# Three edits in the SSD part of a float32 trunk: a borrowed bank for the sums of squares, one output piece in another place, and phase buffers 64 bytes lower

## The chip, the cores and the metric

The kernel runs on one core of one Trainium2 chip. The metric is the device time of one execution in microseconds (us); three runs of the kernel before gave a median of 1430.0 us (1429.96 to 1431.1). PE is the matrix engine TensorE, PEld its weight loads, DVE is VectorE, ACT is ScalarE, POOL is GpSimd, SP is SyncE, which issues the DMAs.

## The reference

Two layers over 512 tokens of width 1024 in float32; the first mixes tokens with an SSD (Mamba-2), the second with an HGRN2. After each mixer come a layer norm, a squared-ReLU MLP of width 4096, a second layer norm and a gate:

```
for i in range(2):
    mix = ssd_mixer(x, ...) if i == 0 else hgrn2_mixer(x, ...)
    h = layer_norm(ALPHA * x + mix)
    h = layer_norm(ALPHA * h + relu(h @ w1)**2 @ w2)
    x = h + sigmoid(h @ w_gate) * (p[i] @ w_proj)
```

The change lies in the SSD mixer. It projects x to z, xs, B, C and dt; xs, B and C pass through a causal convolution of width 4 and a silu. With 32 heads of 64 values in 4 groups, and chunks of 128 tokens:

```
y = y_diag + y_off + d_skip * xs           # products within a chunk, and from the state before it
y = y * silu(z)
y = rms_norm(y, over each group of 512 values) * norm_w
mix = y @ w_out
```

## The kernel before, in words

**Numbers.** Each float32 operand of a large product is split into two parts, hi and lo, of a reduced type that the matrix engine reads at full speed, and a product is three matmuls: hi*hi, hi*lo, lo*hi (`mm3`, L116 to L118). A weight (`unit`) is 128 x 1024: SP loads it into one of three `raw` buffers, ACT casts it to `whi` (L110), DVE subtracts to get `wlo` (L112); there are six `whi` and six `wlo` buffers. The activations that the products read lie in the nine large buffers of pool `b8` (in the profile they are called `b`), or, in the MLP, in tiles called `blk`. In the profile `out<-moving,stationary` names the two operands of a matmul: the stationary one has been loaded into the array, the moving one streams through.

**Phases.** The program goes through four phases: ssd, mlp0, hgrn, mlp1. Each opens a pool of scratch buffers at the same SBUF address (`begin`). Ahead of it in the layout lies `pad`, 64 bytes per partition that nothing reads; one GpSimd memset fills it at the start. So all phase buffers start at byte 173568 of a partition, which is a multiple of 512. The `blk` tiles are the first two buffers of the mlp phases (173568 and 181760). The buffers of `b8`, `whi`, `wlo`, `raw` and the accumulator all start 192 bytes past a multiple of 256.

**PSUM.** Eight banks: four for `pj` (projections, output pieces), one `pt`, two `py0` and `py1`, one `pm`.

**The SSD loop.** Heads are worked on in 16 tiles j of 128 rows (two heads), in pairs. `x_part(j)` projects a tile of xs (24 matmuls) and runs the convolution on it: ACT L570, three DVE instructions L573 that all read the bank, ACT's Silu L574. `z_part(j)` projects a tile of z and takes its Silu (L622). `turn_pair(k)` transposes the two xs tiles of pair k on PE (L639) into `pt` and `pm`; DVE L643 and L647 read them. `decays` prepares the decay factors (ACT's Exp, DVE L663 to L670), `states` the chunk states (L679, DVE L681 to L686). `mixed(j)` makes the tile's y in `py0` (even j) or `py1` (odd j) (L696, L698), and `finish(j)` reads that bank (DVE L714), multiplies by silu(z), splits and adds to the sum of squares `ss` of its group (L724).

When a group g of four tiles is finished, `rms_group(g, bank)` sums `ss` over its rows with four small matmuls (L729; eight records in the profile), ACT takes a square root from the bank (L731), DVE the reciprocal `ri` (L732). `pieces(g, ri)` is a generator of eight output pieces; a piece is 12 matmuls into a fresh `pj` bank, and DVE L250 scales it by `ri` and adds it to `acc`, after which the bank is free. `some(n)` draws n pieces. In iterations k = 3, 5 and 7 (of 1 to 8), `x_part` of tiles 2k and 2k+1 comes first, then `rms_group` with a fourth `pj` bank, then in k = 3 and 5 four pieces at once. In k = 7 there follow z_part(12), mixed(12), mixed(13) and turn_pair(7); the eight pieces of that group are drawn in k = 8, four after z_part(15) and four after the last `mixed`.

**Order.** PE's order in this part is as written (a manual schedule). Within each other engine a scheduler orders the instructions by priorities, where a `high_priority` offset pulls a block ahead of its place (`LEAD` 100, `SOON` 40, `SUMS` for the block sums of the MLP). In the MLP `weight_sums` (L311) loads eight tiles `r` and forms sums of weight blocks on DVE (L323 to L329); the lead of the first such block is `SUMS[0]`.

Of the kernel before, what the change touches and what calls it, by code (L numbers as in the profile page):

```python
# [15 lines left out]
P = 128  # L16
# [13 lines left out]
TURN = 200  # L30

PERIODS = ("TTTTTTTT",) + 3 * ("TTQTQTQTQTQTQTQ",) + ("QQQQQQQ",)
SUMS = (150, 300, 300, 300)

JOBS = "q0 q1 v0 q2 q3 g0 q4 q5 v1 q6 q7 g1 o".split()
LEADIN = 6.0
# [5 lines left out]
def trunk(ctx: ExitStack, tc, a):  # L42
    nc = tc.nc
    pool = lambda name, bufs, **kw: ctx.enter_context(tc.tile_pool(name=name, bufs=bufs, **kw))
# [5 lines left out]
    accp = pool("accp", 1)  # L50
    w4 = pool("w4", 2)
    sm = pool("sm", 2)
    pad = pool("pad", 1)
    psj = pool("psj", 4, space=PSUM)
    pst = pool("pst", 1, space=PSUM)
    psy = pool("psy", 1, space=PSUM)
# [4 lines left out]
    def nm(s):  # L61
        uid[0] += 1
        return f"{s}_{uid[0]}"

    def mk(p, shape, tag, dt=F32, **kw):
        return p.tile(list(shape), dt, tag=tag, name=nm(tag), **kw)
# [9 lines left out]
    def begin(name):  # L76

        if phase:
            phase[1].__exit__(None, None, None)
            phase.clear()  # L80
        phase.append(tc.tile_pool(name=name, bufs=1, reuse_waits="tile"))
        phase.append(phase[0].__enter__())
        phase.reverse()
        phase.append(bufs[name])

    def tmp(tag, shape, dt=F32):
        return mk(phase[0], shape, tag, dt, bufs=phase[2].get(tag, 1))

    def bank(p, tag):
        return mk(p, [P, T], tag)  # L90
# [8 lines left out]
    def unit(src, lead=LEAD):  # L99
        n = src.shape[1]  # L100
        with tc.high_priority(offset=lead):
            raw = mk(raws, [P, 1024], "raw")
            nc.sync.dma_start(raw[:, :n], src)
        return split(raw[:, :n], lead)
# [33 lines left out]
            mm3(ps[:m, tok], hi[:, c], lo[:, c], xs.h(k, tok), xs.l(k, tok), k == 0, k == 7)  # L138


    nc.gpsimd.memset(mk(pad, [P, 16], "pad"), 0.0)
    begin("ssd")
    acc = mk(accp, [P, NCH, D], "acc")

# [93 lines left out]
    def out_part(units, n, xs, c, h, first, scale, last=False, sums=None):  # L238


        sl = slice(c * P, (c + 1) * P)
        ps = bank(psj, "pj")
        for k in range(n):
            hi, lo = units[k // 2]
            ks = slice((k % 2) * 512, (k % 2 + 1) * 512)
            mm3(ps, xs.h(k, sl), xs.l(k, sl), hi[:, ks], lo[:, ks], k == 0, k == n - 1)
        d = acc[:, c, h * 512 : (h + 1) * 512]
        with tc.high_priority(offset=SOON if last else 0):
            if scale is not None:
                nc.vector.scalar_tensor_tensor(d, ps, scale[:, c : c + 1], d, ALU.mult, ALU.add)  # L250
            elif sums is not None:
                nc.vector.tensor_tensor_reduce(d, ps, d, 1.0, 0.0, ALU.add, ALU.add, sums[:, c, h : h + 1])
            elif first:
                nc.vector.scalar_tensor_tensor(d, d, ALPHA, ps, ALU.mult, ALU.add)
            else:
                nc.vector.tensor_add(d, ps, d)
# [125 lines left out]
    def mlp_and_gate(layer, h_s, last):  # L382
# [35 lines left out]
        for g, period in enumerate(PERIODS):  # L418
            if g < 4:
                tiles = hidden(g)  # L420
            if g > 0:
# [8 lines left out]
                w = [[[w2[8 * g - 8 + 4 * i + 2 * j + u] for u in range(2)] for j in range(2)] for i in range(2)]  # L430
                products = block_product(w, blocks.pop(g - 1), SUMS[g - 1], g == 1, *((after, lambda: turned(0), sums) if g == 4 else ()))
            for op in period:
# [145 lines left out]
    def projected(i):  # L578

        if i < 2:  # L580
            return first[i]
        ps = bank(psj, "pj")
        project(unit(wssd[i - 2]), x_s, ps)
        return ps

    def bc_group(g):
        bcm = []
        for which in range(2):
            ps = projected(10 * g + which)
            t = tmp(("bm", "cm")[which], [P, T])  # L590
            conv_silu(ps, 16 + 4 * which + g, t)
            bcm.append(t)
        return bcm

    def bc_prep(bcm, pt, pc):
        bm, cm = bcm
        for c in range(3):
            nc.tensor.transpose(pt[:, c * P : (c + 1) * P], bm[:, c * P : (c + 1) * P], ident)
        btok = tmp("btok", [P, 3, P])
        nc.scalar.copy(btok, pt[:, : 3 * P].rearrange("p (c n) -> p c n", c=3))  # L600
        for c in range(NCH):
            sl = slice(c * P, (c + 1) * P)
            nc.tensor.matmul(pc[:, sl], bm[:, sl], cm[:, sl], start=True, stop=True)
        cbm = tmp("cbm", [P, T])
        nc.vector.tensor_mul(
            cbm.rearrange("p (c l) -> p c l", c=NCH), pc.rearrange("p (c l) -> p c l", c=NCH), bc(triu, 1, NCH)
        )
        return btok, cbm, cm
# [4 lines left out]
    def x_part(j):  # L613
        ps = projected(10 * (j // 4) + 2 + 2 * (j % 4))
        xs = tmp("xs", [P, T])
        conv_silu(ps, j, xs)
        live[j] = [xs]

    def z_part(j):
        ps = projected(10 * (j // 4) + 3 + 2 * (j % 4))  # L620
        sz = tmp("sz", [P, T])
        nc.scalar.activation(sz, ps, AF.Silu)  # L622
        if j in live:
            live[j].insert(1, sz)
        return sz

    def load_decay(j):
        csb = mk(w4, [P, 2, T], "a")
        nc.sync.dma_start(csb, bass.AP(tensor=csd.tensor, offset=csd.offset + 2 * j * T, ap=[[0, P], [T, 2], [1, T]]))
        decay[j] = csb  # L630
# [95 lines left out]
    def rms_group(g, pr):  # L726

        for c in range(NCH):
            nc.tensor.matmul(pr[:, 64 * c : 64 * c + 64], ss[g][:, c * P : (c + 1) * P], ones_s, start=True, stop=True)  # L729
        ri = mk(sm, [P, NCH], "ri")  # L730
        nc.scalar.activation(ri, pr[:, : 64 * NCH].rearrange("p (c n) -> p c n", c=NCH)[:, :, 0], AF.Sqrt, bias=eps)  # L731
        nc.vector.reciprocal(ri, ri)  # L732
        return ri

    def pieces(g, ri):

        for h in range(2):
            units = [unit(a["wso"][4 * g + 2 * h + i]) for i in range(2)]
            for c in range(NCH):
                out_part(units, 4, ys[g], c, h, False, ri)  # L740
                yield

    outs = iter(())
    bcm = {}

    def some(n):
        for _ in range(n):
            next(outs)
# [3 lines left out]
    with tc.manual_schedule(engines={mybir.EngineType.PE}):  # L752
        bcm[0] = bc_group(0)
        for j in range(2):
            load_decay(j)
            x_part(j)
            z_part(j)
        prep[0] = bc_prep(bcm[0], bank(pst, "pt"), bank(psy, "py0"))
        toks.extend(dt_tail())
        turn_pair(0, (bank(psy, "py1"), bank(psj, "pj")))  # L760
        for k in range(1, 9):
            i, j = 2 * k, 2 * k + 1
            mine, theirs = PIECES.get(k, (0, 0))
            decays(i - 2)
            if k < 8:
                if k in (4, 6):
                    bcm[k // 2] = bc_group(k // 2)
                x_part(i)
            else:
                finish(13, *held[:2], z_part(13))  # L770
                z_part(14)
            states(k - 1)
            decays(i - 1)
            some(mine)
            if k < 8:
                load_decay(i)
                x_part(j)
                load_decay(j)
            if k in (3, 5, 7):
                outs = pieces(k // 2 - 1, rms_group(k // 2 - 1, bank(psj, "pj")))  # L780
            some(theirs)
            if k == 1:
                bcm[1] = bc_group(1)
            elif k < 7:
                z_part(i - 2)
                z_part(i - 1)
            elif k == 7:
                z_part(12)
            else:
                z_part(15)  # L790
                some(4)
            if k == 2:
                nc.sync.dma_start(acc, a["x"])
                for c in range(NCH):
                    nc.vector.tensor_scalar(acc[:, c, :], acc[:, c, :], ALPHA, None, ALU.mult)
            done = [mixed(i - 2), (mixed(i - 1))] if k != 7 else [mixed(12)]
            if k == 7:
                live[13].insert(1, None)
                held = mixed(13)
            if k < 8:  # L800
                if k % 2 == 0:
                    prep[k // 2] = bc_prep(bcm[k // 2], bank(psj, "pj"), bank(psj, "pj"))
                turn_pair(k, (bank(pst, "pt"), bank(psm, "pm")))
            for t, d in enumerate(done):
                finish(i - 2 + t, *d)
        some(4)
    h_s, *after = norm(0)
    out_project(a["wso"][12:16], ys[3], False, *after, scale=rms_group(3, bank(psm, "pm")))
    begin("mlp0")
# [491 lines left out]
```

## Time and profile before

| | |
|---|---|
| median of three runs | 1430.0 us (1429.96 to 1431.1) |
| profiled execution, its own time | 1430.54 us |
| its span, first to last instruction | 1428.5 us |
| PE busy | 1415.3 us (99%), mean granted clock 0.998 |
| weight loads (beside PE) | 1182.2 us (83%) |
| DVE busy | 1023.1 us (72%) |
| ACT busy | 743.9 us (52%) |
| POOL busy | 1.6 us |

PE is the bound nearly throughout, so what can be gained is either a wait of PE, or time that its matmuls take beyond their usual rate. Durations of single matmuls overlap in the record: the time that one costs is read from start to start.

### The profile page before, as it was taken

The numbers are of one execution on the slowest core, as the hardware profiler recorded it, in microseconds if no ns is written. First come the engines' busy times: TensorE is split into PE (matmuls) and PEld (weight loads), VectorE is DVE, ScalarE is ACT, GpSimd is POOL, SyncE is SP. The second block draws the span as 40 slices with busy tenths as digits, with TensorE's granted clock in tenths as the row PEclk, the third lists the DMA queues.
The fourth block names the chain that finished last, engine by engine and source line by source line (L and its number), as shares of the span: only waits on it lengthen the run. The fifth ranks groups of instructions, "written<-read, shape, count | busy, mean of one in ns | idle before, by whom it ended". The sixth has DMA issues, their size and how long they took to land.

```text
span 1428.5 us, 20283 instructions
## 1 busy us (share of the span) xinstructions
PE 1415.3 (99%) x8063; PEld 1182.2 (83%) x8063; DVE 1023.1 (72%) x1673; ACT 743.9 (52%) x1089; POOL 1.6 (0%) x9
## 2 busy tenths in 40 slices
PE   9999999999999999999999999999999999999998
PEld 7888888878888888888888888888898888888887
DVE  7997877686967768576864774776785867667873
ACT  7885565573255454545543445464455444543641
POOL 0000000000000000000000000000000000000000
PEclk9999999999999999999999999999999999999999
DMA  8523333323434444443422222222163444444231
GB/s 290 169 99 118 105 103 118 104 89 109 171 104 133 142 128 156 135 148 118 142 94 76 90 93 85 89 77 88 58 236 106 147 141 140 147 133 162 89 118 45
DMA packets 48958, 174.81 MB, mean 122 GB/s; under 512 B 5728, under 2 KB 6368, under 8 KB 48736
## 3 DMA queue, kind: packets, MB, share of 16 engines
q1 hardware_dynamic: 48864, 173.52, 36.5%
q8 instruction: 63, 1.03, 0.3%
q14 instruction: 31, 0.25, 0.1%
HBM read 171.34 MB, written 2.16 MB: 121 GB/s over the span
## 4 chain that ended last, share of the span: by engine, by line
PE 93%; DVE 3%; ACT 2%; DMA 1%; issue 0%; SPq 0%; DVEq 0%; ACTq 0%
PE pj L116 24%; PE pj L117 24%; PE pj L118 24%; PE py L116 5%; PE py L117 5%; PE py L118 5%; PE py L696 1%; PE py L960 1%; DVE wlo L112 1%; PE py L698 1%; DMA a<-csd 1%; PE pt L679 0%; PE pt L230 0%; DMA acc<-in_xw 0%; PE pm L230 0%
## 5 line engine op out<-in xcount | busy, mean ns | idle before, releaser
L110 ACT CAST whi<-raw 128x1024 fp32r<-128x1024 f32 x226 | 237.0, 1050 | 400.1 <-PE pj L117 277.8
L112 DVE TENSOR_TENSOR wlo<-raw,whi 128x1024 fp32r<-128x1024 f32 x226 | 274.8, 1221 | 200.9 <-ACT whi L110 196.1
L116 PE MATMUL pj<-b,whi 128*128 128x512 f32 (+1 forms) x1008 | 381.9, 379 | 0.2 <-ACT b L235 0.2
L117 PE MATMUL pj<-b,whi 128*128 128x512 f32 (+1 forms) x1008 | 379.6, 377 | 0.7 <-DVE b L236 0.7
L118 PE MATMUL pj<-b,wlo 128*128 128x512 f32 (+1 forms) x1008 | 379.3, 376 | 0.0
L116 PE MATMUL pj<-whi,b 128*128 128x512 f32 (+1 forms) x584 | 228.9, 392 | 2.3 <-ACT ri L731 2.2
L118 PE MATMUL pj<-whi,b 128*128 128x512 f32 (+1 forms) x592 | 229.3, 388 | 0.0
L117 PE MATMUL pj<-wlo,b 128*128 128x512 f32 (+1 forms) x584 | 226.0, 387 | 0.0
L117 PEld LDWEIGHTS pj<-b,whi 128*128 128x128 f32 x1008 | 190.2, 189 | 35.0 <-DVE b L236 0.9
L118 PEld LDWEIGHTS pj<-b,wlo 128*128 128x128 f32 x1008 | 190.2, 189 | 34.7
L116 PEld LDWEIGHTS pj<-b,whi 128*128 128x128 f32 x1008 | 189.8, 189 | 35.0 <-ACT b L235 0.5
L116 PEld LDWEIGHTS pj<-whi,b 128*128 128x128 f32 x584 | 109.7, 188 | 26.1 <-ACT ri L731 3.1
L118 PEld LDWEIGHTS pj<-whi,b 128*128 128x128 f32 x592 | 111.2, 188 | 22.8 <-DVE b L1155 0.2
L117 PEld LDWEIGHTS pj<-wlo,b 128*128 128x128 f32 x584 | 109.8, 188 | 21.3
L110 ACT CAST whi<-r 128x1024 fp32r<-128x1024 f32 x64 | 67.1, 1049 | 65.0 <-PE pj L118 36.8
L112 DVE TENSOR_TENSOR wlo<-r,whi 128x1024 fp32r<-128x1024 f32 x64 | 78.1, 1220 | 21.0 <-ACT whi L110 21.0
L118 PE MATMUL py<-whi,b 128*128 128x512 f32 x216 | 84.1, 389 | 0.0
L117 PE MATMUL py<-wlo,b 128*128 128x512 f32 x192 | 74.7, 389 | 0.0
L116 PE MATMUL py<-whi,b 128*128 128x512 f32 x192 | 74.4, 389 | 0.0
L573 DVE SCALAR_TENSOR_TENSOR cv<-pj,cst,cv 128x509 f32<-128x509 f32 (+2 forms) x66 | 48.9, 742 | 2.9 <-ACT cv L570 2.5
L118 PEld LDWEIGHTS py<-whi,b 128*128 128x128 f32 x216 | 40.6, 188 | 8.5
L116 PEld LDWEIGHTS py<-whi,b 128*128 128x128 f32 x192 | 36.1, 188 | 7.6
(335 smaller groups left out, 1811.6 us busy)
## 6 DMA issues: line engine op xcount, KB each, us to landing
raw<-in_w SPq DMA_DIRECT2D x112, 512.0 KB, 3.3
r<-in_w SPq DMA_DIRECT2D x64, 512.0 KB, 3.7
raw<-in_wssd SPq DMA_DIRECT2D x38, 512.0 KB, 4.0
a<-csd SPq DMA_DIRECT2D x16, 512.0 KB, 3.7
raw<-in_wso SPq DMA_DIRECT2D x16, 512.0 KB, 4.2
raw<-in_wg SPq DMA_DIRECT2D x16, 512.0 KB, 3.3
raw<-in_whvg SPq DMA_DIRECT2D x16, 512.0 KB, 3.4
raw<-in_whq SPq DMA_DIRECT2D x16, 512.0 KB, 3.3
```

The costliest lines, as they stand in the source:

```text
L110: nc.scalar.copy(hi[:, :n], f)
L112: nc.vector.tensor_sub(lo[:, :n], f, f32(hi[:, :n]))
L116: nc.tensor.matmul(out, sh, mh, start=start, stop=False, **kw)
L117: nc.tensor.matmul(out, sh, ml, start=False, stop=False, **kw)
L118: nc.tensor.matmul(out, sl, mh, start=False, stop=stop, **kw)
L573: nc.vector.scalar_tensor_tensor(cv[:, d:], ps[:, : T - d], convw[:, i, k : k + 1], cv[:, d:], ALU.mult, ALU.add)
L696: nc.tensor.matmul(yd[64 * r : 64 * r + 64, sl], xdt[:, c, r, :], m[:, r, sl], start=True, stop=c == 0)
L698: nc.tensor.matmul(yd[64 * r : 64 * r + 64, sl], pv[:, c - 1, r, :], ecs[:, r, (c - 1) * P : c * P], start=False, stop=True,)
L960: nc.tensor.matmul(ps[r][32 * b : 32 * b + 32, base + n * c : base + n * c + n], kk[r][:, ts], moving(r, 4 * c + b), start=True, stop=True,)
```

## The change

Four edits, in the order of the diff:

1. `SUMS[0]` goes from 150 to 60: in both MLPs the first block sums get a smaller lead in the scheduler.
2. The pool `pad` and its memset go: every phase's buffers start at 173504, 64 bytes lower, 192 bytes past a multiple of 256.
3. In k = 3, 5 and 7 `rms_group` writes to bank `py0`, which the next `mixed` of an even tile writes later, instead of a `pj` bank.
4. In k = 7 one piece is drawn between z_part(12) and mixed(12), and the last draw is three pieces instead of four.

```
-SUMS = (150, 300, 300, 300)
+SUMS = (60, 300, 300, 300)
...
-    pad = pool("pad", 1)
...
-    nc.gpsimd.memset(mk(pad, [P, 16], "pad"), 0.0)
...
             if k in (3, 5, 7):
-                outs = pieces(k // 2 - 1, rms_group(k // 2 - 1, bank(psj, "pj")))
+                outs = pieces(k // 2 - 1, rms_group(k // 2 - 1, bank(psy, "py0")))
             some(theirs)
...
             elif k == 7:
                 z_part(12)
+                some(1)
             else:
                 z_part(15)
                 some(4)
...
-        some(4)
+        some(3)
     h_s, *after = norm(0)
```

Lines of the changed kernel are one lower from L53 on and two lower from L141 on (L116 becomes L115, L639 becomes L637).

What this does to the order, place by place; the last number behind a name tells one tile from another, and `pj`, `py0` say in which pool's bank it lies. First PE in k = 3, from the last matmul of x_part(7) over the sums of squares to the first piece. Before:

```order
L118 MATMUL pj_182_1094<-b8_6_112,wlo_185_1099 128x512
L729 MATMUL pj_189_1134<-ones_s_20_169,ss_118_734 128x64 x4
L116 MATMUL pj_197_1154<-whi_192_1144,b8_115_727 128x512
L117 MATMUL pj_197_1154<-wlo_193_1146,b8_115_727 128x512
L118 MATMUL pj_197_1154<-whi_192_1144,b8_116_728 128x512
```

PE at the same place after:

```order
L117 MATMUL pj_181_1089<-b8_5_107,wlo_184_1094 128x512
L727 MATMUL py0_188_1129<-ones_s_19_164,ss_117_729 128x64 x4
L115 MATMUL pj_196_1149<-whi_191_1139,b8_114_722 128x512
L116 MATMUL pj_196_1149<-wlo_192_1141,b8_114_722 128x512
L117 MATMUL pj_196_1149<-whi_191_1139,b8_115_723 128x512
```

No row moves; the sums lie in `py0`, so when the pieces begin, the `pj` bank that the sums held stands free for one of them. The same holds in k = 5.

Next PE in k = 7, from the last matmul of z_part(12) to the first matmuls of z_part(13) (the x-side operand of z_part is in `b8`, that of a piece, `b8_344` and `b8_345`, holds a group's finished y). Before:

```order
L118 MATMUL pj_443_2614<-b8_6_112,wlo_446_2619 128x512
L696 MATMUL py0_448_2647<-b_420_2487,xdt_414_2465 64x128 x4
L698 MATMUL py0_448_2647<-ecs_421_2496,pv_430_2544 64x128 x2
...
L696 MATMUL py1_449_2662<-b_431_2550,xdt_415_2467 64x128 x4
L698 MATMUL py1_449_2662<-ecs_432_2559,pv_430_2544 64x128 x2
...
L639 MATMUL pt_450_2677<-cst_18_165,xs_426_2532 128x128 x4
L639 MATMUL pm_451_2678<-cst_18_165,xs_438_2597 128x128 x4
L116 MATMUL pj_462_2720<-b8_5_111,whi_464_2723 128x512
```

PE at the same place after:

```order
L117 MATMUL pj_442_2609<-b8_5_107,wlo_445_2614 128x512
L115 MATMUL pj_453_2654<-whi_448_2644,b8_344_2055 128x512
L116 MATMUL pj_453_2654<-wlo_449_2646,b8_344_2055 128x512
L117 MATMUL pj_453_2654<-whi_448_2644,b8_345_2056 128x512
...
L116 MATMUL pj_453_2654<-wlo_452_2652,b8_344_2055 128x512
L117 MATMUL pj_453_2654<-whi_451_2650,b8_345_2056 128x512
L694 MATMUL py0_454_2668<-b_419_2482,xdt_413_2460 64x128 x4
L696 MATMUL py0_454_2668<-ecs_420_2491,pv_429_2539 64x128 x2
...
L694 MATMUL py1_455_2683<-b_430_2545,xdt_414_2462 64x128 x4
...
L637 MATMUL pt_456_2698<-cst_17_160,xs_425_2527 128x128 x4
L637 MATMUL pm_457_2699<-cst_17_160,xs_437_2592 128x128 x4
L115 MATMUL pj_468_2741<-b8_4_106,whi_470_2744 128x512
```

Twelve matmuls of a piece (rows L115 to L117 into `pj_453`) now stand between z_part(12) and mixed(12), so that the transposes of turn_pair(7) into `pt` and `pm` come twelve matmuls later; the twelve are missing behind the last `mixed`, ahead of the last sums of squares.

ACT at that place, from the convolution of x tile 15 (`cv_2598`) to its Silu (`xs_2597`). Before:

```order
L570 ACTIVATE cv_2598<-pj_2566,cst_165 128x512
L731 ACT_TABLE_LOAD
L731 ACTIVATE ri_2611<-pj_2606,cst_165 128x4
L622 ACT_TABLE_LOAD
L622 ACTIVATE sz_2645<-pj_2614 128x512
L656 ACT_TABLE_LOAD
L656 ACTIVATE cd_2680<-a_2604 128x8
L574 ACT_TABLE_LOAD
L574 ACTIVATE xs_2597<-cv_2598 128x512
L717 ACTIVATE b_456_2695<-y_2697,cst_165 128x512
```

ACT at the same place after (the same tiles are `cv_2593` and `xs_2592`):

```order
L568 ACTIVATE cv_2593<-pj_2561,cst_160 128x512
L729 ACT_TABLE_LOAD
L729 ACTIVATE ri_2606<-py_440_2601,cst_160 128x4
L620 ACT_TABLE_LOAD
L620 ACTIVATE sz_2640<-pj_2609 128x512
L572 ACTIVATE xs_2592<-cv_2593 128x512
L654 ACT_TABLE_LOAD
L654 ACTIVATE cd_2701<-a_2599 128x8
L665 ACTIVATE ecs_2736<-a_2559 128x768
L109 CAST whi_2917<-raw_2915 128x1024
L715 ACTIVATE b_462_2716<-y_2718,cst_160 128x512
```

The Silu of x tile 15 moves ahead of the Exp of the pair's decays and straight behind the Silu of z tile 12, and a table load between them goes. In the whole program ACT has two rows fewer, both table loads. On DVE the third convolution step of x tile 15, which stood behind L714 of tile 12, now stands ahead of it; in k = 3 and 5 the fourth eviction L250 stands ahead of one `wlo`; further rows change places with neighbours in k = 7 and 8, and one `wlo` with a block sum in mlp1. On SP two loads of output weights move ahead of three loads of projection weights before k = 7, and in each MLP one load goes behind a load of a weight.

More of the change, by code (lines that the diff above doesn't have):

```diff
@@ L32 @@
 PERIODS = ("TTTTTTTT",) + 3 * ("TTQTQTQTQTQTQTQ",) + ("QQQQQQQ",)
-SUMS = (150, 300, 300, 300)
+SUMS = (60, 300, 300, 300)
 JOBS = "q0 q1 v0 q2 q3 g0 q4 q5 v1 q6 q7 g1 o".split()
@@ L52, in trunk @@
     sm = pool("sm", 2)
-    pad = pool("pad", 1)
     psj = pool("psj", 4, space=PSUM)
@@ L138, in project @@
             mm3(ps[:m, tok], hi[:, c], lo[:, c], xs.h(k, tok), xs.l(k, tok), k == 0, k == 7)
-    nc.gpsimd.memset(mk(pad, [P, 16], "pad"), 0.0)
     begin("ssd")
@@ L779, in trunk @@
             if k in (3, 5, 7):
-                outs = pieces(k // 2 - 1, rms_group(k // 2 - 1, bank(psj, "pj")))
+                outs = pieces(k // 2 - 1, rms_group(k // 2 - 1, bank(psy, "py0")))
             some(theirs)
@@ L788, in trunk @@
                 z_part(12)
+                some(1)
             else:
@@ L805, in trunk @@
                 finish(i - 2 + t, *d)
-        some(4)
+        some(3)
     h_s, *after = norm(0)
```

## The prediction

> **What bounds the kernel now.** I read the page's busy shares first, then the list of what PE waits for, then the timeline around each wait, and last the rate of PE's matmuls by form.
>
> ```profile
> PE 1415.3 (99%) x8063; PEld 1182.2 (83%) x8063; DVE 1023.1 (72%) x1673; ACT 743.9 (52%) x1089; POOL 1.6 (0%) x9
> core 0: 1428.5 us, clock 0.998
> ```
>
> PE is busy 1415.3 of 1428.5 us. A change can only take away what PE waits, or make its matmuls quicker. The view of the waits of PE (us in total, times, longest):
>
> ```profile
> PE pm L639 <- ACT xs L574: 2.7, 1, 2.7
> PE pj L116 <- ACT ri L731: 2.2, 2, 1.1
> PE pm L150 <- DVE y L147: 1.1, 1, 1.1
> PE pt L230 <- DVE acc L221: 0.9, 1, 0.9
> ```
>
> The first two rows, three waits, lie where the edits are; the others belong to the layer norms. The timeline of PE (start, duration) at the three, k = 3, k = 5 and k = 7:
>
> ```profile
> 118.17 0.39 PE L118 MATMUL pj<-whi,b 128*128 128x512 f32 x1
> 119.68 0.50 PE L116 MATMUL pj<-whi,b 128*128 128x512 f32 x1 [1.12 <-ACT ri L731]
> ...
> 209.07 0.39 PE L118 MATMUL pj<-whi,b 128*128 128x512 f32 x1
> 210.56 0.50 PE L116 MATMUL pj<-whi,b 128*128 128x512 f32 x1 [1.10 <-ACT ri L731]
> ...
> 303.51 0.66 PE L639 MATMUL pt<-cst,xs 128*128 128x128 f32 x4
> 306.86 0.66 PE L639 MATMUL pm<-cst,xs 128*128 128x128 f32 x4 [2.69 <-ACT xs L574]
> 307.27 0.48 PE L116 MATMUL pj<-b,whi 128*128 128x512 f32 x1
> ```
>
> Undisturbed, 512-column matmuls start every 0.227 us (three steps, two rows left out):
>
> ```profile
> 480.39 0.39 PE L116 MATMUL py<-whi,b 128*128 128x512 f32 x1
> ...
> 481.07 0.39 PE L116 MATMUL py<-whi,b 128*128 128x512 f32 x1
> ```
>
> So a piece of 12 takes 2.72 us. From start to start k = 3 shows 1.51 us and k = 5 1.49 us: stalls of 1.28 and 1.26 us. In k = 7 a transposing record of four costs 0.41 us (306.86 to 307.27), and 3.35 us pass: a stall of 2.94 us. Behind that one the clock falls, as the stretches show (length, PE, PEld, DVE, ACT and POOL busy, granted clock, DMA):
>
> ```profile
> 299.00:303.00 4.00, 4.00 (x57) 3.49 (x57) 3.62 (x6) 3.94 (x6) 0.00 (x0) 1.00 0.61 227
> 303.00:307.00 4.00, 1.31 (x17) 0.90 (x14) 3.90 (x13) 3.94 (x6) 0.00 (x0) 1.00 0.00 0
> 307.00:311.00 4.00, 4.00 (x14) 3.25 (x14) 3.96 (x9) 3.97 (x6) 0.00 (x0) 0.62 0.02 4
> ```
>
> z_part(13) and z_part(14) are 48 matmuls from 307.27 to the start of the last at 319.67:
>
> ```profile
> 319.67 0.39 PE L118 MATMUL pj<-b,wlo 128*128 128x512 f32 x1
> ```
>
> 12.40 us for 47 steps, where 47 x 0.2267 = 10.65 would do: 1.75 us lost to the clock.
>
> **The change part by part.** *Sums of squares in py0, k = 3 and 5.* The third piece waits for the bank that the sums held until ACT's square root has read it. That read is late because ACT is busy with other work and then loads a table:
>
> ```profile
> 118.07 1.28 ACT L731 ACT_TABLE_LOAD   x1
> 119.36 0.26 ACT L731 ACTIVATE ri<-pj,cst 128x4 f32<-128x4 f32 x1
> 121.08 0.75 DVE L573 SCALAR_TENSOR_TENSOR cv<-pj,cst,cv 128x511 f32<-128x511 f32 x1
> ...
> 210.24 0.26 ACT L731 ACTIVATE ri<-pj,cst 128x4 f32<-128x4 f32 x1
> 211.00 0.75 DVE L573 SCALAR_TENSOR_TENSOR cv<-pj,cst,cv 128x511 f32<-128x511 f32 x1
> ```
>
> Nothing is added or removed, so the four pieces want four banks of which x tiles 2k and 2k+1 hold two until their third convolution step. Now the last piece takes the bank of x tile 2k+1. In k = 3 the second piece's last matmul starts at 118.17, the third could follow at 118.40 and the fourth at 121.1; but the step ends at 121.08 + 0.75 = 121.83 and PE could start at about 121.9: a new wait of 0.8 us on DVE L573. Before, the fourth started at 119.68 + 2.72 and 0.1 for the slow first step, 122.5, so the gain is 0.6, not 1.28. In k = 5 the third could start at 209.30 and the fourth at 212.0, and the step ends at 211.75: no wait; the gain is the whole stall, 1.3 us. Together 1.9, with the slow first steps that go too 2.0. Bounds: 1.3 if DVE's step in k = 5 slips by 0.7, 2.5 if both stalls go. The bank py0 costs nothing: its last reader was done before the sums (L724 of the group's last tile precedes them), and the next mixed comes behind four pieces.
>
> *One piece ahead of mixed(12), k = 7.* pm's transposes wait for the Silu of x tile 15, the last of a chain in ACT and DVE:
>
> ```profile
> 299.87 1.28 ACT L731 ACT_TABLE_LOAD   x1
> 301.44 1.28 ACT L622 ACT_TABLE_LOAD   x1
> 302.74 0.60 ACT L622 ACTIVATE sz<-pj 128x512 f32<-128x512 f32 x1
> ...
> 304.88 1.28 ACT L574 ACT_TABLE_LOAD   x1
> 306.18 0.63 ACT L574 ACTIVATE xs<-cv 128x512 f32<-128x512 f32 x1
> ...
> 302.10 0.75 DVE L714 SCALAR_TENSOR_TENSOR y<-xs,cst,py 128x512 f32<-128x512 f32 x1
> ```
>
> The piece moves PE's arrival at pm from 303.92 to 306.6. In the new order the Silu stands no longer behind two table loads and the Exp: it follows sz (302.74 + 0.60), at 303.4, and is done by 304.0; its convolution step now takes the place of L714 at 302.10 or an earlier one and is done by 302.9. Slack 2.6 us; even if the Silu stayed at its old place (done at 306.8), a wait of only 0.2 would be left. So the stall of 2.94 us goes, and with it the 1.75 of the clock if the stall is what let it fall: 4.69. The piece itself moves, from behind the last mixed: no cost, except where it was cover. That cover hides the last tiles' finish ahead of the last sums of squares:
>
> ```profile
> 337.63 0.66 PE L696 MATMUL py<-b,xdt 128*64 128x128 f32 x8
> 351.89 1.00 PE L729 MATMUL pm<-ones_s,ss 128*128 128x64 f32 x8
> ...
> 340.40 0.74 DVE L714 SCALAR_TENSOR_TENSOR y<-xs,cst,py 128x512 f32<-128x512 f32 x1
> 347.98 0.68 DVE L724 TENSOR_TENSOR ss<-ss,sq 128x512 f32<-128x512 f32 x1
> ```
>
> From L714 to the end of L724 are 8.26 us, of which 0.7 is an eviction that now comes earlier. The mixed pair starts 4.0 us sooner (6.7 gained, 2.72 given to the piece), tile 14's bank is full some 1.8 us behind that (335.4), the chain ends at about 343.1 and PE arrives at 351.89 - 6.7 = 345.2: 2 us spare. What is late next is the layer norm: 1.1 and 0.9 us in the list, unchanged and moved rigidly. On SP the two output weights go ahead of projection weights; the list has no wait of PE for a DMA, so nothing.
>
> By the Trainium skill (TensorE: Matmul & The Clock Gate, "Part 1: The HAM clock gate") the clock is halved after a whole idle window of about 3.4 us, and a stall of 2.94 us is shorter. By that rule the loss at 307 to 311 would have another cause and could stay, and the sum would be 1.75 us smaller. The rows decide: the stretch right behind the longest stall is the one below full clock, while the stalls of 1.3 us are followed by none.
>
> *64 bytes lower.* The matmuls on `blk`, the first two buffers of the phase pool, are slower than others of the same form (median durations, then the starts):
>
> ```profile
> L116 PE MATMUL pj<-whi,blk x64: 393/398/401, 469.3 to 1335.0; 128*128 128x512 f32 x64
> 469.32 0.40 PE L116 MATMUL pj<-whi,blk 128*128 128x512 f32 x1
> ...
> 470.72 0.40 PE L116 MATMUL pj<-whi,blk 128*128 128x512 f32 x1
> ```
>
> From the first to the last row are six steps in 1.40 us, 0.2333 each, against 0.2267: 6.6 ns. There are six such groups of 64 (L116, L117, L118, into pj and into py), 384 matmuls: 2.5 us. The `b8` blocks, with the same layout, weights and banks, differ in the address alone: 192 past a multiple of 256, where `blk` starts at a multiple of 512. After the change `blk` too is 192 past a multiple of 256 (though 448, not 192, past one of 512). Whether the address is the cause, no run shows yet. Bounds: 0 (it is the region, or the 512 decides) and 2.5. I take 2.5, since the new remainder is that of every quick operand.
>
> *SUMS[0], the memset.* The order shows one block sum changing place with one `wlo`; the list of PE's waits has none for L323 to L329. The memset ran on POOL, busy 1.6 us in all. Both nothing; a late block sum could cost one weight's DVE step, 1.2 us:
>
> ```profile
> L112 DVE TENSOR_TENSOR wlo<-r,whi 128x1024 fp32r<-128x1024 f32 x64 | 78.1, 1220 | 21.0 <-ACT whi L110 21.0
> ```
>
> Sum: 2.0 + 4.7 + 2.5 = 9.2. The profiled execution took 1430.54 (span 1428.5), 0.5 above the median, so 1421.3 against it and 1420.8 against the median.
>
> **The rivals.** *Stalls go, `blk` stays slow* (region, not address): 1430.0 - 6.7 = 1423.3. For it: only one pair of addresses was seen. Against it: the slowness is uniform over both MLPs, so it is tied to the place.
>
> *The k = 7 stall moves or the clock does not recover.* DVE and ACT are busy 3.9 of every 4 us from 303 on, so a PE that is ahead may meet them again at states(7), mixed(14) or the last sums. If the clock's 1.75 stays: 1422.5 with `blk` mended, 1425 without. If 2 us of spare at the end prove to be minus 1, the same. Against it: the chain loses two table loads, 2.56 us of ACT.
>
> *The change does not do it:* the new order of DVE in k = 7 puts the first eviction, which waits for the piece, ahead of the decays; if that holds mixed(14) by 5 us or more, k = 7 is worth nothing, and with `blk` unchanged the whole is 1428 to 1430, within 0.2%. For it: DVE has no free tenth there. Against it: the piece ends by 303.0, so the eviction would wait 0.1 us.
>
> *Slower.* The new address is worse than the old. 384 matmuls would have to lose the stalls' 6.7 and 2.9 more, 9.6 us: 25 ns each, 0.252 from start to start. That is the point from which it decides; at 30 ns each it ends at 1430.0 - 6.7 + 11.5 = 1434.8. Against it: the two rates seen are 0.227 and 0.233, 6.6 ns apart, with no third.
>
> **How the numbers follow.** Both terms, 1420.8: 0.58. `blk` unchanged, 1423.3: 0.25. Stall moved or clock lost, 1422.5 to 1426: 0.10. Nothing: 0.05. Slower: 0.02. About 0.2%, 2.9 us, is what a measurement of this kernel tells from no change: faster means below 1427.1. Faster 0.92, same 0.06, slower 0.02. Range: 1419.0 (k = 3's stall goes wholly, 0.5, and the ends of the clock and layer norms a little better) to 1425.0, the second case and half of the third.
>
> **What would show it.** Right: no row "PE pj L115 <- ACT ri" and none "PE pm L637 <- ACT xs" among PE's waits; a new one of about 0.9 us for DVE L571 at 121; full clock from 300 to 312; ACT's Silu of tile 15 straight behind sz; starts on `blk` every 0.227 us; the waits of the layer norms as before. Wrong: a wait of over 1 us between 300 and 350 for DVE or ACT, `blk` at 0.233 or worse, or a stretch below full clock in the SSD part.

## The result and the profile after

| | before | after |
|---|---|---|
| median | 1429.89 us (1428.01 to 1431.1, six runs) | 1421.22 us (1420.58 to 1421.61, six runs) |
| profiled execution, its span | 1430.54, 1428.5 us | 1421.14, 1419.0 us |
| PE busy | 1415.3 us | 1410.8 us |

The ratio is 0.994 with a 95% interval of 0.9927 to 0.9953: 8.7 us less. The waits of PE in the changed kernel (us in total, times, longest):

```profile
PE pm L148 <- DVE y L145: 1.1, 1, 1.1
PE pt L228 <- DVE acc L219: 0.9, 1, 0.9
PE pj L116 <- DVE b L234: 0.7, 1, 0.7
PE pj L115 <- DVE cv L571: 0.7, 1, 0.7
```

Both rows that led the list before, for ACT's `ri` and for the Silu in k = 7, are gone. The fourth row is new; on the timeline of PE it is the fourth piece of k = 3:

```profile
120.20 0.39 PE L117 MATMUL pj<-whi,b 128*128 128x512 f32 x1
121.26 0.47 PE L115 MATMUL pj<-whi,b 128*128 128x512 f32 x1 [0.68 <-DVE cv L571]
```

1.06 us from start to start is a stall of 0.83. In k = 7, PE's two transposes of the pair and the first matmul behind them, and then ACT up to the Silu of x tile 15:

```profile
303.71 0.66 PE L637 MATMUL pt<-cst,xs 128*128 128x128 f32 x4
304.20 0.60 PE L637 MATMUL pm<-cst,xs 128*128 128x128 f32 x4
304.56 0.47 PE L115 MATMUL pj<-b,whi 128*128 128x512 f32 x1
...
298.63 0.26 ACT L729 ACTIVATE ri<-py,cst 128x4 f32<-128x4 f32 x1
300.21 0.60 ACT L620 ACTIVATE sz<-pj 128x512 f32<-128x512 f32 x1
300.70 0.62 ACT L572 ACTIVATE xs<-cv 128x512 f32<-128x512 f32 x1
```

The Silu is done at 301.3, 2.9 us ahead of the transposes into `pm`. The stretch behind runs at full clock (same columns as before; the number behind the last count is the clock, here 1.00):

```profile
303.00:307.00 4.00, 4.00 (x35) 3.40 (x30) 4.00 (x11) 3.40 (x5) 0.00 (x0) 1.00 0.02 4
```

And the matmuls on `blk`, the first of its groups and two starts six steps apart:

```profile
L115 PE MATMUL pj<-whi,blk x64: 388/389/397, 462.0 to 1325.7; 128*128 128x512 f32 x64
462.04 0.39 PE L115 MATMUL pj<-whi,blk 128*128 128x512 f32 x1
...
463.40 0.39 PE L115 MATMUL pj<-whi,blk 128*128 128x512 f32 x1
```

1.36 us for six steps, 0.227 each. Laying the PE records of both traces side by side by their position, the lead of the changed kernel grows so: 0.7 us by 70 us, 1.15 by 139 (k = 3 lies between), 2.5 by 217 (k = 5), 7.1 by 325 (k = 7), 7.3 by 394, 8.6 by 744 (mlp0), 8.2 by 787, 8.4 by 1145, 9.5 at the end (mlp1). The first 0.7 is gained before the first of the edits: the row "PE py L116 <- ACT whi L169", 0.8 us in the list of before, is absent here. In the runs below it is 0.3 to 0.6 us in four and absent in the other eight, with the memset and without it, so it belongs to none of the edits.

### The profile page after: what moved, and what is told of

Read it like the earlier page. It is cut to its first block, busy times and chain, and to the rows that moved or that the text cites. A ratio compares the mean times of both kernels' runs of the same rounds, so it can differ in the third digit from the quotient of the medians.

```text
span 1419.0 us, 20283 instructions
## 1 busy us (share of the span) xinstructions
PE 1410.8 (99%) x8063; PEld 1181.4 (83%) x8063; DVE 1022.9 (72%) x1673; ACT 741.5 (52%) x1087; POOL 1.6 (0%) x8
## 4 chain that ended last, share of the span: by engine, by line
PE 95%; DVE 2%; ACT 2%; issue 1%; DMA 0%; ACTq 0%
PE pj L115 24%; PE pj L116 24%; PE pj L117 24%; PE py L117 5%; PE py L116 5%; PE py L115 5%; PE py L694 1%; PE py L959 1%; PE py L696 1%; DVE wlo L111 1%; ACT whi L109 1%; PE pt L677 0%; PE pt L228 0%; DVE cv L571 0%; PE pm L228 0%
## 5 line engine op out<-in xcount | busy, mean ns | idle before, releaser
L115 PE MATMUL pj<-b,whi 128*128 128x512 f32 (+1 forms) x1008 | 381.1, 379 | 0.2 <-ACT b L233 0.2
L116 PE MATMUL pj<-b,whi 128*128 128x512 f32 (+1 forms) x1008 | 378.8, 376 | 0.7 <-DVE b L234 0.7
L117 PE MATMUL pj<-b,wlo 128*128 128x512 f32 (+1 forms) x1008 | 378.7, 376 | 0.0
L115 PE MATMUL pj<-whi,b 128*128 128x512 f32 (+1 forms) x584 | 228.8, 392 | 0.7 <-DVE cv L571 0.7
L117 PE MATMUL pj<-whi,b 128*128 128x512 f32 (+1 forms) x592 | 229.2, 388 | 0.0
L116 PE MATMUL pj<-wlo,b 128*128 128x512 f32 (+1 forms) x584 | 225.9, 387 | 0.0
L116 PEld LDWEIGHTS pj<-b,whi 128*128 128x128 f32 x1008 | 189.8, 188 | 34.8 <-DVE b L234 0.9
L117 PEld LDWEIGHTS pj<-b,wlo 128*128 128x128 f32 x1008 | 189.7, 188 | 34.6
L115 PEld LDWEIGHTS pj<-b,whi 128*128 128x128 f32 x1008 | 189.5, 188 | 34.4 <-ACT b L233 0.5
L117 PEld LDWEIGHTS pj<-whi,b 128*128 128x128 f32 x592 | 111.2, 188 | 22.8 <-DVE b L1154 0.2
L115 PEld LDWEIGHTS pj<-whi,b 128*128 128x128 f32 x584 | 109.7, 188 | 24.0 <-ACT cd L654 1.1
L116 PEld LDWEIGHTS pj<-wlo,b 128*128 128x128 f32 x584 | 109.8, 188 | 21.3
L117 PE MATMUL py<-whi,b 128*128 128x512 f32 x216 | 84.1, 389 | 0.0
L116 PE MATMUL py<-wlo,b 128*128 128x512 f32 x192 | 74.7, 389 | 0.0
L115 PE MATMUL py<-whi,b 128*128 128x512 f32 x192 | 74.4, 389 | 0.0
L571 DVE SCALAR_TENSOR_TENSOR cv<-pj,cst,cv 128x509 f32<-128x509 f32 (+2 forms) x66 | 49.2, 746 | 2.7 <-ACT cv L568 2.4
L117 PEld LDWEIGHTS py<-whi,b 128*128 128x128 f32 x216 | 40.5, 188 | 8.5
L115 PEld LDWEIGHTS py<-whi,b 128*128 128x128 f32 x192 | 36.0, 188 | 7.6
```

The lines of the kernel that those rows point to most:

```text
L115: nc.tensor.matmul(out, sh, mh, start=start, stop=False, **kw)
L116: nc.tensor.matmul(out, sh, ml, start=False, stop=False, **kw)
L117: nc.tensor.matmul(out, sl, mh, start=False, stop=stop, **kw)
L571: nc.vector.scalar_tensor_tensor(cv[:, d:], ps[:, : T - d], convw[:, i, k : k + 1], cv[:, d:], ALU.mult, ALU.add)
```

## The experiments

All are versions of the changed kernel, timed in three groups beside the kernel before, whose median was 1430.31, 1429.49 and 1430.02 us. Ratios are to those.

**The pad back.**

```
+    pad = pool("pad", 1)
...
+    nc.gpsimd.memset(mk(pad, [P, 16], "pad"), 0.0)
```

> The changed kernel with the 64-byte pad put back, all orders the same. Theory A (the address of blk sets the rate): the 384 matmuls on blk start every 0.233 us again instead of 0.227, 2.5 us are lost, about 1423.8 us. Theory B (the quicker blk came with something else, such as the other orders): starts stay at 0.227, 1421.2 us.

Measured: 1423.68 us (1423.11 to 1424.01), ratio 0.9954 (0.9942 to 0.9967). Apart from the memset the orders of all engines are those of the changed kernel; `blk` is slow again:

```profile
L116 PE MATMUL pj<-whi,blk x64: 393/394/402, 462.3 to 1328.0; 128*128 128x512 f32 x64
```

The 64 bytes are the cause, and they are worth 2.5 us.

**No piece ahead of mixed(12).**

```
                 z_part(12)
-                some(1)
...
-        some(3)
+        some(4)
```

> The changed kernel without the piece ahead of mixed(12), four pieces again behind the last mixed. In its order ACT's Silu of x tile 15 still stands straight behind sz of tile 12, ahead of the Exp. Theory A (the piece is what hides the chain to the Silu): pm's transposes wait about 2.7 us again, the clock falls, 1421.2 + 4.7 = 1425.9 us. Theory B (the new place of the Silu is what matters, by the rows it is done at the moment PE arrives): a wait of under 0.4 us, full clock, 1421.2 to 1421.6 us.

Measured: 1422.01 us (1421.7 to 1423.36), ratio 0.9945 (0.9932 to 0.9957): 0.8 us more than with the piece, not 4.7. The Silu's wait does not return. In its place stands another, in the list and on the timeline of PE, with ACT's row beside it:

```profile
PE py L694 <- ACT ri L729: 1.1, 1, 1.1
...
297.77 0.39 PE L117 MATMUL pj<-b,wlo 128*128 128x512 f32 x1
299.25 0.66 PE L694 MATMUL py<-b,xdt 128*64 128x128 f32 x8 [1.09 <-ACT ri L729]
...
298.93 0.26 ACT L729 ACTIVATE ri<-py,cst 128x4 f32<-128x4 f32 x1
```

mixed(12) writes `py0`, and ACT has not read the sums out of it yet: the wait for `ri` has followed the bank. So this is what the piece covers, 1.25 us from start to start. The wait also lets the Silu get ahead: it ends at 301.62 and the transposes into `pm` start at 302.95, so without the 1.25 us PE would come just as the Silu is done.

**The sums back in a pj bank.**

```
-  rms_group(k // 2 - 1, bank(psy, "py0"))
+  rms_group(k // 2 - 1, bank(psj, "pj"))
```

> The changed kernel with the sums of squares back in a pj bank. Theory A: the waits of the third piece for ACT's ri return in k = 3 and 5 (about 1.1 us each) and the wait for DVE L571 in k = 3 goes: 1421.2 + 1.9 = 1423.1 us, k = 7 as in the changed kernel. Theory B (in k = 7 the piece now finds no free bank before ri is read): a further wait of about 1 us there, 1424.2 us.

Measured: 1422.86 us (1422.24 to 1424.7), ratio 0.9952 (0.9939 to 0.9966), 1.6 us more. The list of waits has

```profile
PE pj L115 <- ACT ri L729: 2.2, 2, 1.1
```

for k = 3 and 5, and the row for DVE L571 is gone; k = 7 is as in the changed kernel. This is Theory A.

**Sums of k = 7 in py1, no piece.** As the second run, with `bank(psy, "py1" if k == 7 else "py0")`. `py1` is written 1.6 us later than `py0`, by mixed(13).

> The changed kernel without the piece, and with the sums of k = 7 in py1 instead of py0 (k = 3 and 5 keep py0). Its order on ACT in k = 7 is that of the kernel before: the Silu of x tile 15 behind the Exp and two table loads. Theory A (that order alone made the wait of k = 7): pm's transposes wait 2.7 us again, the clock falls behind it, 1421.2 + 4.5 = 1425.7 us. Theory B (the wait came from the bank of the sums): no wait, 1421.2 us.

Measured: 1424.98 us (1423.69 to 1426.18), ratio 0.9968 (0.9956 to 0.9979). The old order on ACT brings the old wait (first the list of PE's waits, then rows of DVE and ACT up to the Silu of x tile 15):

```profile
PE pm L637 <- ACT xs L572: 2.7, 1, 2.7
...
300.53 0.74 DVE L571 SCALAR_TENSOR_TENSOR cv<-pj,cst,cv 128x511 f32<-128x511 f32 x1
...
301.10 1.28 ACT L654 ACT_TABLE_LOAD   x1
302.63 1.28 ACT L572 ACT_TABLE_LOAD   x1
303.92 0.63 ACT L572 ACTIVATE xs<-cv 128x512 f32<-128x512 f32 x1
```

The last convolution step on DVE is done at 301.27, and the Silu starts only at 303.92: what stands between on ACT is the Exp of the decays with the two table loads. Beside the second run only the bank differs, and the scheduler's answer to it: there ACT's Silu stands ahead of the Exp, here behind, and rows on DVE change places too. In the profiled execution the clock does not fall (length and busy times as before, clock 1.00), although the stall is 2.92 us long:

```profile
301.00:305.00 4.00, 1.32 (x16) 0.92 (x11) 3.90 (x15) 3.94 (x6) 0.00 (x0) 1.00 0.00 0
305.00:309.00 4.00, 4.00 (x21) 3.32 (x20) 3.97 (x10) 3.97 (x6) 0.00 (x0) 1.00 0.05 13
```

Of the six executions two have a mean clock of 1.000 and spans of 1421.6 and 1421.9 us; the other four have 0.998 or 0.999 and 1422.9 to 1424.2. So the same stall costs its 2.9 us, and mostly, not always, 1 to 2.5 us on top. Of those four no trace was kept, so that their clock fell behind this stall is inferred. For the three at 0.998 it is firm, since no execution of a kernel without this stall is that low; 0.999 is found in such kernels too. The kernel before shows both as well: 13 of its 31 executions in the three groups are at 0.998, with 1429.5 to 1430.9 us, and the nine below 1429 us are all at 0.999 or 1.000.

**The Silu first, no piece.** As the run above, with the convolution of x tile 15 under `tc.high_priority(offset=60)`; ACT's order is then `ri`, Silu of x tile 15, sz, Exp.

> As the run with the sums in py1 and no piece, but the convolution of x tile 15 has priority, so that ACT's Silu of it stands behind ri and ahead of sz and the Exp. Theory A (the order on ACT is the whole of k = 7's gain, the piece gives nothing more): wait at pm under 0.1 us, full clock, 1421.2 us. Theory B (the 2.7 us of cover by the piece are needed beside it): a wait of 1 us or more at pm or at mixed, 1422.2 us or more.

Measured: 1420.75 us (1420.53 to 1421.64), ratio 0.9940 (0.9928 to 0.9953). PE goes from one transpose to the next without a wait:

```profile
300.48 0.63 ACT L573 ACTIVATE xs<-cv 128x512 f32<-128x512 f32 x1
...
301.25 0.66 PE L638 MATMUL pt<-cst,xs 128*128 128x128 f32 x4
301.74 0.60 PE L638 MATMUL pm<-cst,xs 128*128 128x128 f32 x4
```

The order alone, without the piece, brings all of k = 7's gain. The priority pulls DVE's steps of this convolution forward as well; that it is ACT's order that counts follows from the rows of the run above, where DVE was done 2.65 us before the Silu began. 1420.75 against 1421.22 is within the spread of either, so this version is as quick as the changed kernel, with one edit less in the order of PE, and not shown to be quicker.

**Six matmuls into the wait.** As the run with the sums in `py1`, and in turn_pair(7):

```
+  if (k, t) == (7, 1):
+      junk = bank(psj, "pj")
+      for n in range(6):
+          nc.tensor.matmul(junk, ys[2].h(n % 4, slice(0, P)), ys[2].h(n % 4), start=n == 0, stop=n == 5)
```

> As the run with the sums in py1 and no piece, with six 512-column matmuls (1.36 us) whose result nothing reads between the transposes into pt and those into pm of k = 7. Theory A (it is the long stall that lets the clock fall): the stall shrinks from 2.9 to 1.6 us, the clock stays full, and the kernel is 1.7 us quicker than without the six matmuls though it does more: about 1424.0 us. Theory B (the clock falls there for another reason): the six matmuls hide in the wait and the time stays, 1425.7 us.

Measured: 1424.66 us (1424.47 to 1425.82), ratio 0.9968 (0.9956 to 0.9981). The stall is 1.46 us,

```profile
304.64 0.66 PE L641 MATMUL pm<-cst,xs 128*128 128x128 f32 x4 [1.30 <-ACT xs L572]
```

and the mean clock is 1.000 in all six executions, against two of six without the fillers. The time hardly shows it: 0.3 us less in the medians, with ranges that overlap, and in the profiled executions a layer norm wait ("PE pt L228 <- DVE acc L219") is 1.4 us here and 0.9 there. The two executions without the fillers that kept the clock took 1423.7 and 1423.9 us, less than any with them. That a stall of half the length spares the clock fits the twelve clocks, and the times do not settle it.

**The fourth piece of k = 3 between z_part(4) and z_part(5).**

```
-            some(theirs)
+            some(theirs - (k == 3))
...
                 z_part(i - 2)
+                some(int(k == 3))
                 z_part(i - 1)
```

> The changed kernel with the fourth piece of k = 3 drawn between z_part(4) and z_part(5) instead of ahead of both. Theory A (in k = 3 the fourth piece only waits for the bank of x tile 7, and nothing else is late there): the wait of 0.85 us for DVE L571 goes, 1420.4 us. Theory B (z_part(4) then takes that bank and waits for the same step): no change, 1421.2 us.

Measured: 1421.33 us (1421.24 to 1422.17), ratio 0.9945 (0.9932 to 0.9957), no change. z_part(4) now waits for the same bank:

```profile
120.60 0.39 PE L117 MATMUL pj<-whi,b 128*128 128x512 f32 x1
121.66 0.47 PE L115 MATMUL pj<-b,whi 128*128 128x512 f32 x1 [0.67 <-DVE cv L571]
```

Whatever comes fourth needs the bank of x tile 7: with four `pj` banks the wait belongs to the convolution, not to the piece.

**SUMS[0] back to 150.**

> The changed kernel with SUMS[0] back at 150. Theory A (the lead of the first block sums moves one wlo on DVE and one load on SP in mlp1, and PE waits for neither): 1421.2 us. Theory B (a late weight): up to 1.2 us in either direction.

Measured: 1421.14 us (1420.38 to 1421.41), ratio 0.9941 (0.9927 to 0.9955): nothing, as in Theory A.

**The address.** The other four vary where the buffers start: a pad ahead of all of them, or pads of 128, 32 and 192 bytes ahead of the phases.

> The changed kernel with 64 bytes ahead of all weight, activation and phase buffers: b8, whi, wlo and blk all start at multiples of 256 (blk of 512). Theory A (a stationary operand at a multiple of 256 is slow by itself): all 512-column matmuls with such a stationary operand, some 5000, lose 6.6 ns each, 33 us, about 1454 us. Theory B (it is slow only where stationary and moving operand stand differently within 256 bytes): nothing is slow, 1421 us. Theory C (only buffers in the phase region can be slow): blk alone is slow, 1423.8 us.

> The changed kernel with a pad of 128 bytes: blk starts 64 past a multiple of 256, whi and wlo stay at 192. Theory A (stationary and moving operand must agree within 128 bytes): starts on blk every 0.227 us, 1421.2 us. Theory B (they must agree within 256 bytes): every 0.233 us, 1423.7 us.

> The changed kernel with a pad of 32 bytes: blk starts 224 past a multiple of 256, 32 bytes from whi and wlo. Theory A (any difference within the period costs): starts on blk every 0.233 us, 1423.7 us. Theory B (only a difference of 64 bytes or more costs): every 0.227 us, 1421.2 us.

> The changed kernel with a pad of 192 bytes: blk starts 128 past a multiple of 256, 64 bytes below whi and wlo in it. Theory A (only the difference to the moving operand within 128 bytes counts): as slow as with the 64-byte pad, 0.233 us, 1423.7 us. Theory B (a stationary operand at a multiple of 256 is what is slow, and the run with all buffers 64 higher hid it in some other way): 0.227 us, 1421.2 us.

Measured, with the mean step between the starts of matmuls on `blk` (some 380 steps each), and where `blk` (stationary) and `whi`, `wlo` (moving) start, modulo 256:

| kernel | blk | whi, wlo | step, ns | median, us |
|---|---|---|---|---|
| before | 0 | 192 | 233.3 | 1429.89 |
| changed | 192 | 192 | 226.8 | 1421.22 |
| pad back (64) | 0 | 192 | 233.3 | 1423.68 |
| all 64 higher | 0 | 0 | 226.8 | 1421.11 |
| pad 128 | 64 | 192 | 232.9 | 1423.71 |
| pad 32 | 224 | 192 | 233.1 | 1423.40 |
| pad 192 | 128 | 192 | 229.3 | 1421.50 |

The medians of the last four rows are of four, three, three and two executions.

The one row of the page for `pj<-whi,blk` in the run with all buffers 64 higher, where `blk` starts at a multiple of 512 just as before:

```profile
L116 PE MATMUL pj<-whi,blk x64: 388/389/397, 462.2 to 1325.5; 128*128 128x512 f32 x64
```

So it is not the address of `blk` by itself (Theory A of that run falls by 33 us), nor the region. Where `blk` and the weights that stream past it start alike within 256 bytes, the step is 226.8 ns, twice out of twice, as it is for `b8`; where they differ it is 233, three layouts of four, and 32 bytes of difference are enough. The fourth, `blk` at 128, has three rates at one pair of remainders: a step takes 229.1 ns from a matmul of L116 (`whi` streams, the hi part of `blk` is loaded), 231.8 from one of L117 (`wlo`, the same part) and 226.0, the quick rate, from one of L118 (`whi`, the lo part). So the two remainders within 256 bytes are not the whole rule. The expectation of that run fits neither theory, and what the difference does inside the chip stays open.

## Why the prediction was right

**The sum.** 9.2 us were forecast against the profiled execution and 9.4 came (1430.54 to 1421.14), of which the start of the program gave about 0.7 that belongs to none of the edits. So 8.7 are theirs, as in the medians, and that the total comes so close to the forecast is in part luck.

**k = 3 and 5.** Forecast 0.6 and 1.3, by positions 0.45 and 1.4. The new wait was named with its place and its engine, 0.8 us forecast, 0.83 from start to start.

**k = 7.** Forecast 4.7, by positions 4.5. The size came out right, but the step that explained it is only half borne out. The prediction gave the piece the gain, since it moves PE's arrival by 2.72 us, and took the new order on ACT for a second help. The runs show that the order on ACT is enough: without the piece the Silu's wait stays away (0.8 us lost, for another reason), and with neither the piece nor the new order it is there. Whether the piece would have been enough by itself is open: no run has it with the old order, where the prediction's rows leave a wait of 0.2 us. That order is the scheduler's answer to an edit elsewhere: it stands in the run with `py0` and no piece and in the one with the piece and a `pj` bank, and not in the one with `py1` and no piece; why the scheduler answers so, no run shows. What the piece itself does was missed: it covers the read of `ri` out of the borrowed bank. The prediction said that `py0` "costs nothing" since the next mixed comes behind four pieces; in k = 7 only z_part(12) stands between, and without the piece mixed(12) waits 1.25 us.

**The clock.** The 1.75 us were read from one execution, in which it had fallen. The run with the old wait shows the same stall with a lowered clock in four executions of six, by their mean clocks and spans. The term should have been entered as a chance: some 1.2 us in the mean of these six. The kept traces show what the chance hangs on. In the one of the kernel before the clock changes at 307.96, 311.37 and 1427.53 us, which are 1 and 327 times 3.413 us apart. In the one with the old wait it falls at 1422.48, after the program's last instruction; counted back from there in the same steps, an edge lies at 302.91, inside the stall. The stretches between such edges, two of the kernel before, then two of that run:

```profile
304.54:307.96 3.42, 1.10 (x7) 1.01 (x8) 3.38 (x14) 3.36 (x6) 0.00 (x0) 1.00 0.00 0
307.96:311.37 3.41, 3.41 (x10) 2.65 (x9) 3.41 (x8) 3.40 (x4) 0.00 (x0) 0.50 0.08 26
...
302.91:306.33 3.42, 1.72 (x10) 1.51 (x11) 3.39 (x14) 3.39 (x5) 0.00 (x0) 1.00 0.02 5
1422.48:1424.00 1.52, 0.00 (x0) 0.00 (x0) 0.00 (x0) 0.00 (x0) 0.00 (x0) 0.50 0.00 0
```

In the kernel before PE works 1.10 us of the first stretch, and the next runs at half clock. In the other run the edge cuts the stall in two, PE still works 1.72 us of the emptier stretch, and the clock stays. Over the fourteen kept traces the clock falls 15 times, 14 of them at the end of the program, each time behind a stretch in which PE works 1.45 us or less; behind none with 1.72 us or more does it fall. So, by these traces, whether a stall of 2.9 us costs the clock depends on where it lies between the edges; what happens from 1.45 to 1.72 us no run shows. By the Trainium skill (TensorE: Matmul & The Clock Gate, "Part 1: The HAM clock gate") the clock is judged in windows of about 3.4 us that run free of the program. The steps of 3.413 us agree with that. That a whole window must be idle, as the Trainium skill has it there, does not agree: in the kernel before, 1.10 us of work in the window did not keep the clock up.

**64 bytes.** Forecast 2.5, and 2.5 came, with the pad alone as with the lead in the two MLPs (1.3 and 1.1 to 1.3). The argument by remainders modulo 256 was right for this kernel, but for a reason that it did not give: as far as the layouts tried show, the remainder has to be that of the moving operand, not that of "every quick operand".

**SUMS[0], the memset, the last sums.** Nothing, as forecast: 1421.14 us with `SUMS[0]` back, and 1421.11 with a memset of the same size in the run with all buffers 64 higher. At the last sums the chain ends at 342.25 and PE arrives at 344.84:

```profile
341.56 0.69 DVE L722 TENSOR_TENSOR ss<-ss,sq 128x512 f32<-128x512 f32 x1
...
344.84 1.00 PE L727 MATMUL pm<-ones_s,ss 128*128 128x64 f32 x8
```

2.6 us to spare, where 2 were forecast.

## What to carry to other kernels

When a scheduler orders an engine, an edit of a bank or of one step on another engine can turn its order round at a place that the diff doesn't touch, and that can be worth more than the edit: compare the orders, and try the order alone. A borrowed buffer takes its wait along: ask who writes it next, and how much work stands between. Compare the start-to-start time of matmuls of one form but different buffers; a difference of a few ns that is the same everywhere can be a matter of layout, and here it was had back by leaving out a buffer that nothing reads.

## What the runs showed of the hardware

A 512-column matmul of this type takes 226.8 ns from start to start where its stationary and its moving operand start alike within 256 bytes of a partition (192 and 192, 0 and 0), and 233 ns with a stationary operand at 0, 64 or 224 and a moving one at 192; 128 and 192 gave three rates from 226.0 to 231.8, 229.3 in the mean. The effect is the same in both MLPs and in every run with the same layout, and moving all buffers together by 64 bytes leaves the step at 226.8 ns. A stall of PE of 2.9 us may or may not be followed by a stretch at reduced clock, in one and the same program: in the traces here the clock fell where PE worked 1.45 us or less between two edges 3.413 us apart, and not where it worked 1.72 us or more.
